# A stated order for top-k, gate softmax, transposes and first router products in a decoder-block kernel

## The chip, the cores and the metric

The kernel runs on one core of one Trainium2 chip. The metric is the time of one execution on the device in microseconds, and the median of several runs is compared. The kernel before takes 1516.3 us (median of 3 runs, 1514.54 to 1518.07).

## What is computed

One decoder block on 512 tokens of width 1024. A joint input projection feeds a gated short convolution and a differential attention; one output projection and a layer norm follow. Behind them stands the channel mixer, a retrieval of 16 out of 16,384 experts for each of 8 heads, and a last layer norm. The change touches the channel mixer alone. Its core, for a chunk of 128 tokens:

```
q = (xc @ wq).reshape(PEER_CHUNK, PEER_HEADS, 2, PEER_DHALF)
sc = jnp.einsum('chpd,hpnd->chpn', q, keys)
s1, i1 = lax.top_k(sc[:, :, 0], PEER_TOPK)
s2, i2 = lax.top_k(sc[:, :, 1], PEER_TOPK)
cand = s1[..., :, None] + s2[..., None, :]             # 16 x 16 per head
cidx = i1[..., :, None] * PEER_NKEYS + i2[..., None, :]
top_s, pos = lax.top_k(cand, PEER_TOPK)
eidx = jnp.take_along_axis(cidx, pos, axis=-1)
g = jax.nn.softmax(top_s, axis=-1)
act = jax.nn.gelu(jnp.einsum('chkd,cd->chk', u[eidx], xc))
return jnp.einsum('chk,chkd->cd', g * act, v[eidx])
```

## The kernel before

The program has four stages: the input projection with attention and convolution, the output projection with the layer norm, the scores against the keys, and the channel mixer. Matrix products that need full precision are made as three products of a high and a low part: ScalarE casts the high part (L72), another engine subtracts for the low part (L73).

The channel mixer treats three of the four token chunks (384 tokens) densely: it computes all 16,384 experts and multiplies by a gate matrix that is zero where an expert wasn't chosen. The fourth chunk gathers its experts' rows. The parts that matter here:

- **Top-k** (`topk`, VectorE). First part: for 8 heads and 2 halves the 16 best of 128 (`top16`, L270 to L274). Second part, from the sums of both halves: the 16 best candidates of each head, the subtraction of the largest (gx, L299), the exp on ScalarE (L300), its sum, reciprocal and product (L302 to L304), then the two index numbers of each choice, found with comparisons and a tree of additions on tiles of 128x2048 (L309 to L331). It is called for chunks 0, 1 and 2 ahead of the expert blocks. The scores of the third chunk come back from DRAM, where ScalarE's evacuations (scst, L409) and stores (L410) have put them.
- **Expert blocks, first half** (`dense_u`, 128 of them). Each loads a weight block of 128x1024, casts it (whi, ScalarE), makes the low part (wlo, on GpSimd for the first NPOOL = 14 blocks, on VectorE for the others), runs 24 products of 128x384 on TensorE into a PSUM tile psH (two buffers) and applies GELU on ScalarE (hs, L432). The results wait in 42 buffers; with two more blocks in psH, 44 blocks can be worked on ahead of the second half.
- **Transposes** (`topk_transpose`): index numbers and gates of a chunk are transposed on TensorE (psX, L337) and evacuated; an edge of the order puts them behind block 3, 10 and 14 (the table TK).
- **Router** (L455 to L473, 24 groups of 16 tokens). VectorE makes one-hot tiles from index numbers and gates (oa, bl, bh, each with two buffers, L462 to L465), TensorE forms 32 products of 128x128 (psG, L470 and L471), ScalarE scales the result into a tile stg, and a transfer stores it in DRAM (G_D, L473).
- **Second half** (`dense_w`, `dense_v`). It reads the gate matrix back from G_D (gt, L553), loads v (vr, L540), multiplies gates and hidden values and accumulates 18 products of 128x512 per block in PSUM tiles acc. The other blocks of the first half stand between them.

A scheduler of the language sets the order of the instructions on each engine from the program's text and from edges that the text adds with `issue_after`; each engine then works through its own list in that order. The transfers of the weights, of v and of the gate matrix stand on SyncE's queue; the stores of G_D and of the scores stand on ScalarE's.

Of the kernel before, what the change touches and what calls it, by code (L numbers as in the profile page):

```python
# [9 lines left out]
F32 = mybir.dt.float32  # L10
# [3 lines left out]
U32 = mybir.dt.uint32  # L14
AF = mybir.ActivationFunctionType
ALU = mybir.AluOpType
AX = mybir.AxisListType
# [7 lines left out]
PH = 8  # L25
# [3 lines left out]
ND = 384  # L29
NDC = 3  # L30
# [7 lines left out]
HS_BUFS = 42  # L38
NPOOL = 14
TAIL = 4  # L40
VR = 3
WB = 4
GA = 4
TK = ((0, 3), (3, 10), (10, 14))
GI2 = 8
# [8 lines left out]
def build(nc, tc, I, out, dbg=None):  # L54
# [13 lines left out]
    SC_D = [dram.tile([128, 16, 128], F32, name=f"SC_D{j}") for j in range(2)]  # L68
# [193 lines left out]
    scs = {}  # L262
# [5 lines left out]
    def top16(tk, vals, pos, src, n):  # L268
        t = tk.tile([128, 128], F32, name="rest", bufs=2)
        nc.vector.max(vals[:, 0:8], src)  # L270
        nc.vector.max_index(pos[:, 0:8], vals[:, 0:8], src)  # L271
        nc.vector.match_replace(t[:, 0:n], vals[:, 0:8], src, -3.0e38)  # L272
        nc.vector.max(vals[:, 8:16], t[:, 0:n])
        nc.vector.max_index(pos[:, 8:16], vals[:, 8:16], t[:, 0:n])  # L274

    def topk(tk, sc, nb):
        m = tk.tile([128, 2, PH, 16], F32, name="m", bufs=nb)
        ix = tk.tile([128, 2, PH, 16], U32, name="ix")
        for h in range(PH):
            for p in range(2):  # L280
                top16(tk, m[:, p, h, :], ix[:, p, h, :], sc[:, 2 * h + p, :], 128)
        ixf = tk.tile([128, 2, 16, PH], F16, name="ixf")
# [12 lines left out]
        for h in range(PH):  # L295
            top16(tk, tsc[:, h, :], pos[:, h, :], cand[:, h, :], 112)
        g = tk.tile([128, 16, PH], F32, name="g", bufs=nb)
        gx = tk.tile([128, PH, 16], F32, name="gx")
# [6 lines left out]
        u1 = tk.tile([128, PH, 16], U32, name="u1")  # L305
        u2 = tk.tile([128, PH, 16], U32, name="u2")
        ab = tk.tile([128, 2, 16, PH], F16, name="ab")
# [3 lines left out]
        nc.vector.scalar_tensor_tensor(abv[:, 0], u2, 12.0, u1, op0=ALU.subtract, op1=ALU.max)  # L311
        u3 = tk.tile([128, PH, 16], U32, name="u3")
        u4 = tk.tile([128, PH, 16], U32, name="u4")
        nc.vector.tensor_scalar(u3, pos, 12, None, op0=ALU.bitwise_and)
        nc.vector.tensor_scalar(u4, pos, 3, None, op0=ALU.bitwise_and)
        nc.vector.scalar_tensor_tensor(u3, pos, 64.0, u3, op0=ALU.is_lt, op1=ALU.mult)
        nc.vector.tensor_tensor(abv[:, 1], u3, u4, op=ALU.add)
        idf = tk.tile([128, 2, 128], F32, name="idf", bufs=nb)
# [9 lines left out]
        for n in (8, 4, 2):  # L328
            nc.vector.tensor_tensor(e[:, :, 0:n], e[:, :, 0:n], e[:, :, n:2 * n], op=ALU.add)  # L329
        nc.vector.tensor_tensor(idf, e[:, :, 0], e[:, :, 1], op=ALU.add)  # L330
        return idf, g  # L331

# [93 lines left out]
    def dense_u(j):  # L426
        uh, ul = wblock(I["uT"][j], nc.gpsimd if j < NPOOL else nc.vector)
        ps = psH.tile([128, S], F32, name="psH")
        for k in range(NK):
            mm = mm3(ps[:, 0:ND], uh[:, k, :], ul[:, k, :], x1h[:, k, 0:ND], x1l[:, k, 0:ND], k == 0, k == NK - 1)  # L430
        hs = hsp.tile([128, ND], F32, name="hs")
        nc.scalar.activation(hs, ps[:, 0:ND], AF.Gelu)  # L432
        hidden[j] = hs
        return mm

    picked = []
    for c in range(NDC):
        if c == 2:
            scs[c] = tk.tile([128, 16, 128], F32, name="sc", bufs=2)
            nc.sync.dma_start(out=scs[c], in_=SC_D[0])  # L440
        picked.append(topk(tk, scs[c], 2))
    for c in range(NDC):
# [12 lines left out]
    for tb in range(NTG):  # L455
# [39 lines left out]
    def gather_steps():  # L495
        with tc.issue_after(gate):
            idf, g = topk(t3, sc3, 1)
        for p in range(2):
# [153 lines left out]
```

## Time and profile before

| What | Value |
|---|---|
| Median of 3 runs | 1516.3 us (1514.54 to 1518.07) |
| Profiled execution | 1515.57 us, its span 1513.8 us |
| Mean granted clock of TensorE | 0.985 |
| DMA, mean over the span | 248 GB/s |

The span is the time between the first and the last instruction of the profiled execution; the remaining 1.8 us lie around it. A busy share is the time in which an engine had an instruction in work, over the span. The engines are PE (TensorE), PEld (its weight loads), DVE (VectorE), ACT (ScalarE), POOL (GpSimd) and SP (SyncE). In the page's slices the channel mixer begins in the tenth of 40 slices, at some 360 us, and its second half in the seventeenth, at some 626 us.

### The profile page before, as it was taken

The numbers are of one execution on the slowest core, as the hardware profiler recorded it, in microseconds if no ns is written. First come the engines' busy times: TensorE is split into PE (matmuls) and PEld (weight loads), VectorE is DVE, ScalarE is ACT, GpSimd is POOL, SyncE is SP. The second block draws the span as 40 slices with busy tenths as digits, with TensorE's granted clock in tenths as the row PEclk, the third lists the DMA queues.
The fourth block names the chain that finished last, engine by engine and source line by source line (L and its number), as shares of the span: only waits on it lengthen the run. The fifth ranks groups of instructions, "written<-read, shape, count | busy, mean of one in ns | idle before, by whom it ended". The sixth has DMA issues, their size and how long they took to land.

```text
span 1513.8 us, 22123 instructions
## 1 busy us (share of the span) xinstructions
PE 1452.1 (96%) x8097; PEld 1299.5 (86%) x8097; DVE 1183.8 (78%) x2373; ACT 592.9 (39%) x932; POOL 476.7 (31%) x322
## 2 busy tenths in 40 slices
PE   7999988997799999899999999999999999999996
PEld 5787867997798999888989999899899999998985
DVE  4546545579999887699888888888888888888745
ACT  3544244452345555334433333333333333333342
POOL 1000043674430000000345454445444544444200
PEclk9999999999899999999999999999999999999999
DMA  6111263454436666996799999999999999999731
GB/s 254 62 65 58 96 208 131 156 197 131 139 130 228 242 233 250 298 295 193 264 377 339 350 334 346 344 333 344 334 357 329 350 333 344 334 340 346 275 126 70
DMA packets 146429, 375.94 MB, mean 248 GB/s; under 512 B 16272, under 2 KB 63376, under 8 KB 142992
## 3 DMA queue, kind: packets, MB, share of 16 engines
q1 hardware_dynamic: 100960, 203.97, 39.8%
q0 software_dynamic: 36864, 134.23, 24.3%
q10 hardware_dynamic: 8496, 36.32, 6.3%
q8 instruction: 63, 1.03, 0.3%
q14 instruction: 46, 0.38, 0.1%
HBM read 343.55 MB, written 30.93 MB: 247 GB/s over the span
## 4 chain that ended last, share of the span: by engine, by line
PE 82%; DVE 12%; DMA 3%; ACT 1%; issue 1%; SPq 0%; POOL 0%; ACTq 0%; DVEq 0%; POOLq 0%
PE psH L86 14%; PE psH L84 14%; PE psH L85 14%; PE acc L84 11%; PE acc L85 11%; PE acc L86 11%; PE psG L470 1%; PE psS L180 1%; PE psG L471 1%; DVE rest L272 1%; DVE sc L325 1%; DMA raw<-w_out 1%; DVE sc L329 1%; DVE ix L274 1%; DVE ix L271 1%
## 5 line engine op out<-in xcount | busy, mean ns | idle before, releaser
L84 PE MATMUL psH<-x1Th,whi 128*128 128x384 f32 (+1 forms) x1280 | 423.7, 331 | 15.0 <-ACT hs L432 15.0
L86 PE MATMUL psH<-x1Th,wlo 128*128 128x384 f32 (+1 forms) x1280 | 423.0, 330 | 3.7 <-DVE wlo L73 2.5
L85 PE MATMUL psH<-x1Tl,whi 128*128 128x384 f32 (+1 forms) x1280 | 420.9, 329 | 0.0
L72 ACT CAST whi<-raw 128x1024 fp32r<-128x1024 f32 x200 | 209.7, 1050 | 435.9 <-PE psH L85 313.6
L508 POOL DMA_INDIRECT row<-u,idx x128 | 169.5, 1324 | 457.8 <-ACT hs L432 290.3
L85 PE MATMUL acc<-vl,wh 128*128 128x512 f32 x756 | 294.4, 389 | 0.0
L86 PE MATMUL acc<-vh,wl 128*128 128x512 f32 x756 | 294.3, 389 | 0.0
L84 PE MATMUL acc<-vh,wh 128*128 128x512 f32 x756 | 288.9, 391 | 4.4 <-ACT vh L72 4.4
L84 PEld LDWEIGHTS psH<-x1Th,whi 128*128 128x128 f32 x1280 | 243.9, 191 | 19.3 <-ACT hs L432 15.7
L73 DVE TENSOR_TENSOR wlo<-raw,whi 128x1024 fp32r<-128x1024 f32 x146 | 180.0, 1233 | 92.1 <-ACT whi L72 90.6
L86 PEld LDWEIGHTS psH<-x1Th,wlo 128*128 128x128 f32 x1280 | 243.9, 191 | 5.7 <-DVE wlo L73 3.4
L85 PEld LDWEIGHTS psH<-x1Tl,whi 128*128 128x128 f32 x1280 | 244.1, 191 | 3.2
L73 POOL TENSOR_TENSOR wlo<-raw,whi 128x1024 fp32r<-128x1024 f32 x54 | 136.0, 2522 | 300.7 <-ACT whi L72 299.8
L508 POOL DMA_INDIRECT row<-v,idx x128 | 166.1, 1298 | 183.7 <-DVE x L523 136.2
L72 ACT CAST wh<-hs 128x384 fp32r<-128x384 f32 x128 | 65.6, 514 | 322.1 <-PE acc L85 318.2
L84 PEld LDWEIGHTS acc<-vh,wh 128*128 128x128 f32 x756 | 142.2, 188 | 30.9 <-ACT vh L72 4.8
L86 PEld LDWEIGHTS acc<-vh,wl 128*128 128x128 f32 x756 | 142.0, 188 | 29.0
L73 DVE TENSOR_TENSOR vl<-vr,vh 128x1024 fp32r<-128x1024 f32 x126 | 154.3, 1224 | 16.0 <-ACT vh L72 15.7
L523 DVE SCALAR_TENSOR_TENSOR x<-row,gw,x 128x1024 f32<-128x1024 f32 x128 | 164.0, 1281 | 3.5 <-DMA row<-v,idx 2.6
L85 PEld LDWEIGHTS acc<-vl,wh 128*128 128x128 f32 x756 | 142.0, 188 | 26.0
L516 DVE SCALAR_TENSOR_TENSOR row<-row,x 128x1024 f32<-128x1024 f32 x128 | 154.7, 1221 | 10.7 <-DMA row<-u,idx 10.7
L72 ACT CAST vh<-vr 128x1024 fp32r<-128x1024 f32 x126 | 131.9, 1048 | 0.1
(196 smaller groups left out, 1668.5 us busy)
## 6 DMA issues: line engine op xcount, KB each, us to landing
raw<-uT SPq DMA_DIRECT2D x128, 512.0 KB, 5.4
vr<-v SPq DMA_DIRECT2D x128, 512.0 KB, 5.4
G_D<-stg ACTq DMA_DIRECT2D x24, 1024.0 KB, 4.7
gt<-G_D SPq DMA_DIRECT2D x46, 512.0 KB, 7.9
raw<-wq SPq DMA_DIRECT2D x32, 512.0 KB, 3.4
raw<-w_in SPq DMA_DIRECT2D x24, 512.0 KB, 3.4
raw<-w_out SPq DMA_DIRECT2D x16, 512.0 KB, 4.7
xr<-xT SPq DMA_DIRECT2D x4, 512.0 KB, 6.5
```

The lines of the kernel that those rows point to most:

```text
L72: nc.scalar.copy(out=hi, in_=raw)
L73: return sub.tensor_sub(lo, raw, hi.bitcast(F32))
L84: nc.tensor.matmul(ps, lh, rh, start=first, stop=False)
L85: nc.tensor.matmul(ps, lh, rl, start=False, stop=False)
L86: return nc.tensor.matmul(ps, ll, rh, start=False, stop=last)
L180: nc.tensor.matmul(sp[:, p, 0:w], qz[:, h, p, qs], kT[:, h, 0:w], start=True, stop=False)
L271: nc.vector.max_index(pos[:, 0:8], vals[:, 0:8], src)
L272: nc.vector.match_replace(t[:, 0:n], vals[:, 0:8], src, -3.0e38)
L274: nc.vector.max_index(pos[:, 8:16], vals[:, 8:16], t[:, 0:n])
L508: ins = nc.gpsimd.indirect_dma_start(out=t, out_offset=None, in_=I["uv"[p]], in_offset=bass.IndirectOffsetOnAxis(ap=idx[:, p, k:k + 1], ax ...
L516: nc.vector.scalar_tensor_tensor(t, t, 1.0, x1, op0=ALU.mult, op1=ALU.mult, accum_out=dots[:, k:k + 1])
L523: nc.vector.scalar_tensor_tensor(x1, t, gw[:, k:k + 1], x1, op0=ALU.mult, op1=ALU.add, accum_out=tots[:, GCH:GCH + 1] if k == 127 else None)
```

## The change

The number of blocks whose low part GpSimd makes rises from 14 to 18. The exp of the gates and the sum, reciprocal and product behind it leave `topk` for a function `gates`. For the first two chunks the exps are issued behind the GELU of block 10, sum and product behind the first part of the third chunk's top-k; for the third chunk they come behind block 18 and its own top-k. The transposes are put behind block 12, 13 and 20, and all router products behind the last product of block 18. The first ten blocks now stand in the text between the top-k of the second and of the third chunk. Four index tiles share the memory of ix.

```diff
-NPOOL = 14
+NPOOL = 18
...
-TK = ((0, 3), (3, 10), (10, 14))
+GATES_AT = (10, 18)
+TRANSPOSE_AT = (12, 13, 20)
+ROUTER_AT = 18
...
-    def topk(tk, sc, nb):
-        m = tk.tile([128, 2, PH, 16], F32, name="m", bufs=nb)
+    def topk(tk, sc, nb, between=None):
+        m = tk.tile([128, 2, PH, 16], F32, name="m", bufs=min(nb, 2))
...
+                ins = top16(tk, m[:, p, h, :], ix[:, p, h, :], sc[:, 2 * h + p, :], 128)
+        if between:
+            with tc.issue_after(between(ins)):
+                return topk_rest(tk, sc, nb, m, ix)
+        return topk_rest(tk, sc, nb, m, ix)
...
-        nc.scalar.activation(gx, gx, AF.Exp)
-        gs = tk.tile([128, PH], F32, name="gs")
-        nc.vector.tensor_reduce(gs, gx, axis=AX.X, op=ALU.add)
-        nc.vector.reciprocal(gs, gs)
-        nc.vector.tensor_tensor(g.rearrange("p k h -> p h k"), gx, gs.unsqueeze(2).broadcast_to([128, PH, 16]), op=ALU.mult)
...
+    def gates(tk, gxs, nb, last, exp_after=None):
+        gt = []
+        with tc.issue_after(exp_after) if exp_after else ExitStack():
+            for gx in gxs:
+                nc.scalar.activation(gx, gx, AF.Exp)
+        with tc.issue_after(last.ins):
+            for gx in gxs:
+                g = tk.tile([128, 16, PH], F32, name="g", bufs=nb)
+                gs = tk.tile([128, PH], F32, name="gs", bufs=2)
+                nc.vector.tensor_reduce(gs, gx, axis=AX.X, op=ALU.add)
+                nc.vector.reciprocal(gs, gs)
+                ins = nc.vector.tensor_tensor(g.rearrange("p k h -> p h k"), gx, gs.unsqueeze(2).broadcast_to([128, PH, 16]), op=ALU.mult)
+                gt.append(g)
+        return gt, ins.ins
...
+    picked = [topk(tk, scs[c], NDC) for c in range(2)]
+    scs[2] = tk.tile([128, 16, 128], F32, name="sc", bufs=2)
+    nc.sync.dma_start(out=scs[2], in_=SC_D[0])
+    for j in range(GATES_AT[0]):
+        _, act = dense_u(j)
+    gt = []
+
+    def first_gates(ins):
+        g, last = gates(tk, [gx for _, gx, _ in picked], NDC, ins, act.ins)
+        gt.extend(g)
+        return last
+
+    picked.append(topk(tk, scs[2], NDC, first_gates))
     for c in range(NDC):
-        for j in range(*TK[c]):
-            mm = dense_u(j)
+        for j in range(j + 1, TRANSPOSE_AT[c]):
+            mm, act = dense_u(j)
+            if j == ROUTER_AT - 1:
+                router = mm.ins
+            if j == GATES_AT[1] - 1:
+                gt.extend(gates(tk, [picked[2][1]], NDC, picked[2][2], act.ins)[0])
         with tc.issue_after(mm.ins):
-            topk_transpose(c, *picked[c])
+            topk_transpose(c, picked[c][0], gt[c])
...
-            for t in range(4):
-                q = o0 + t
-                nc.tensor.matmul(ps[:, t, :], oa[:, q, :], bh[:, q, :], start=True, stop=False)
-                nc.tensor.matmul(ps[:, t, :], oa[:, q, :], bl[:, q, :], start=False, stop=True)
+            with tc.issue_after(router):
+                for t in range(4):
+                    q = o0 + t
+                    nc.tensor.matmul(ps[:, t, :], oa[:, q, :], bh[:, q, :], start=True, stop=False)
+                    nc.tensor.matmul(ps[:, t, :], oa[:, q, :], bl[:, q, :], start=False, stop=True)
```

What this does to the lists of the engines is seen at three places.

ScalarE, around the end of the scores. Before, with the exp of the second chunk (gx, L300) ahead of the cast and the last evacuation of scores:

```order
L395 COPY qT<-psH 128x256
L300 ACTIVATE gx<-gx 128x128
L72 CAST whi<-raw 128x1024
L409 COPY scst<-psT 128x512 x2
L410 DMA SC_D_70<-scst 128x512
L410 DMA SC_D_71<-scst 128x512
L432 ACT_TABLE_LOAD
L432 ACTIVATE hs<-psH 128x384
```

With the change, behind the GELU of block 10 (L446 was L432, L336 was L300, L74 was L72):

```order
L446 ACTIVATE hs<-psH 128x384
L336 ACT_TABLE_LOAD
L336 ACTIVATE gx<-gx 128x128 x2
L74 CAST whi<-raw 128x1024
L446 ACT_TABLE_LOAD
L446 ACTIVATE hs<-psH 128x384
```

Both exps now stand behind ten GELUs, with two table loads around them. A place in the list of its own remains to the exp of the third chunk, behind block 18.

VectorE, at the first splits of weights (wlo) that it makes in the channel mixer. Before, for block 15, with one-hots of the router already around it:

```order
L321 TENSOR_TENSOR sc<-ab,iota_1507 128x2048
L304 TENSOR_TENSOR g<-gx,gs 128x8x16
L73 TENSOR_TENSOR wlo<-raw,whi 128x1024
L325 TENSOR_TENSOR sc<-sc,ixf 128x2048
L329 TENSOR_TENSOR sc<-sc 128x2x1024
L462 TENSOR_TENSOR oa<-iox,iT 128x2048
L463 TENSOR_TENSOR bl<-iox,iT 128x2048
L329 TENSOR_TENSOR sc<-sc 128x2x512
L73 TENSOR_TENSOR wlo<-raw,whi 128x1024
```

With the change, for block 19 (L75 was L73, L320, L324 and L328 were L321, L325 and L329):

```order
L320 TENSOR_TENSOR sc<-ab,iota_1507 128x2048
L324 TENSOR_TENSOR sc<-sc,ixf 128x2048
L328 TENSOR_TENSOR sc<-sc 128x2x1024
L75 TENSOR_TENSOR wlo<-raw,whi 128x1024
L328 TENSOR_TENSOR sc<-sc 128x2x512
L328 TENSOR_TENSOR sc<-sc 128x2x256
L329 TENSOR_TENSOR idf<-sc 128x256
L75 TENSOR_TENSOR wlo<-raw,whi 128x1024
```

The first split now stands behind the comparisons, the products and the first addition of the third chunk's tree. Ahead of it one router group's four one-hot operations stand fewer than before.

TensorE, around the last router product (psG) ahead of the second half. Before:

```order
L470 MATMUL psG_5340<-bh_5304,oa_5303 128x128
L471 LDWEIGHTS oa_5303
L471 MATMUL psG_5340<-bl_5305,oa_5303 128x128
L85 MATMUL psH_6237<-x1Tl_1497,whi_6232 128x384
L86 MATMUL psH_6237<-x1Th_1496,wlo_6233 128x384
L84 MATMUL psH_6270<-x1Th_1496,whi_6265 128x384
```

With the change (L496 and L497 were L470 and L471):

```order
L496 MATMUL psG_5526<-bh_5490,oa_5489 128x128
L497 LDWEIGHTS oa_5489
L497 MATMUL psG_5526<-bl_5491,oa_5489 128x128
L86 MATMUL acc0_5547<-vh_6292,wh_6300 128x512
L86 MATMUL acc1_5548<-vh_6292,wh_6300 128x512
L86 MATMUL acc2_5549<-vh_6292,wh_6300 128x512
```

Before, the last 74 expert products of the first half's 44 blocks (1056 products) stand behind the last router product and ahead of the first acc; with the change all 1056 stand ahead of it, and the last 158 router products of 768 stand behind the last expert product. Ahead of the first router product stand 170 expert products before and 432 with the change; the router products stand in 79 runs between expert products before and in 67 with the change.

## Rows read from the trace of the kernel before

**Rows 1.** The page, busy time, share of the span and instructions of each engine:

```profile
PE 1452.1 (96%) x8097; PEld 1299.5 (86%) x8097; DVE 1183.8 (78%) x2373; ACT 592.9 (39%) x932; POOL 476.7 (31%) x322
```

**Rows 2.** Waits of TensorE: engine, line waited for, us in total, times, longest us:

```profile
PE psH L84 <- ACT hs L432: 15.0, 1, 15.0
...
PE psG L470 <- DVE bh L464: 4.2, 1, 4.2
```

**Rows 3.** ScalarE's timeline: start us, us, line, operation, tiles, [idle before <- releaser]:

```profile
378.69 0.31 ACT L300 ACTIVATE gx<-gx 128x128 f32<-128x128 f32 x1 [17.15 <-DVE gx L299]
...
382.67 1.28 ACT L432 ACT_TABLE_LOAD   x1 [1.77 <-DMA SC_D<-scst]
```

**Rows 4.** Windows: us, engines' busy time (count), TensorE's granted clock, DMA share, GB/s:

```profile
384.50:390.00 5.50, 5.49 (x17) 5.50 (x18) 5.50 (x6) 1.28 (x2) 2.82 (x1) 0.50 0.78 302
413.00:417.50 4.50, 4.49 (x19) 4.48 (x19) 4.50 (x12) 0.00 (x0) 0.00 (x0) 0.62 0.34 117
626.00:629.00 3.00, 2.94 (x8) 2.44 (x9) 3.00 (x15) 1.72 (x4) 0.00 (x0) 0.50 1.12 342
```

**Rows 5.** TensorE's timeline, expert products at 360, 390 and 451 to 457 us:

```profile
360.46 0.42 PE L84 MATMUL psH<-x1Th,whi 128*128 128x384 f32 x1
...
390.32 0.34 PE L84 MATMUL psH<-x1Th,whi 128*128 128x384 f32 x1
...
391.19 0.34 PE L86 MATMUL psH<-x1Th,wlo 128*128 128x384 f32 x1
...
450.92 0.45 PE L86 MATMUL psH<-x1Th,wlo 128*128 128x384 f32 x1 [1.53 <-DVE wlo L73]
...
457.32 0.44 PE L86 MATMUL psH<-x1Th,wlo 128*128 128x384 f32 x1 [0.99 <-DVE wlo L73]
```

**Rows 6.** TensorE's timeline, a run of ten router products between two expert products:

```profile
443.24 0.34 PE L85 MATMUL psH<-x1Tl,whi 128*128 128x384 f32 x1
...
443.88 0.22 PE L471 MATMUL psG<-bl,oa 128*128 128x128 f16 x1
...
444.22 0.34 PE L84 MATMUL psH<-x1Th,whi 128*128 128x384 f32 x1
```

**Rows 7.** TensorE's timeline, last router, last expert and first acc product:

```profile
608.51 0.22 PE L471 MATMUL psG<-bl,oa 128*128 128x128 f16 x1
...
621.28 0.34 PE L86 MATMUL psH<-x1Th,wlo 128*128 128x384 f32 x1
...
626.06 1.65 PE L84 MATMUL acc<-vh,wh 128*128 128x512 f32 x3 [4.44 <-ACT vh L72]
```

**Rows 8.** The chain of waits, 608 to 627 us: start us, us, what:

```profile
609.44 4.82 DMA G_D<-stg
...
618.98 4.74 DMA vr<-v
```

**Rows 9.** VectorE's timeline, third chunk's top-k, operations beside GpSimd's, last one-hots:

```profile
330.59 2.40 DVE L309 TENSOR_SCALAR u<-pos 128x128 uint32<-128x128 uint32 x1
...
345.04 2.59 DVE L304 TENSOR_TENSOR g<-gx,gs 128x128 f32<-128x128 f32 x1
...
436.34 2.53 DVE L464 TENSOR_TENSOR bh<-bl,gT 128x2048 f16<-128x2048 f16 x1
...
443.69 0.26 DVE L299 TENSOR_TENSOR gx<-tsc 128x128 f32<-128x128 f32 x1
...
449.44 0.38 DVE L304 TENSOR_TENSOR g<-gx,gs 128x128 f32<-128x128 f32 x1
...
452.03 1.23 DVE L329 TENSOR_TENSOR sc<-sc 128x2048 f16<-128x2048 f16 x1
...
594.67 1.22 DVE L462 TENSOR_TENSOR oa<-iox,iT 128x2048 f16<-128x2048 f16 x1
595.81 1.22 DVE L463 TENSOR_TENSOR bl<-iox,iT 128x2048 f16<-128x2048 f16 x1
```

**Rows 10.** GpSimd's timeline, the split behind its longest pause here:

```profile
380.01 3.28 POOL L73 TENSOR_TENSOR wlo<-raw,whi 128x1024 fp32r<-128x1024 f32 x1 [16.27 <-ACT whi L72]
```

More of the change, by code (lines that the diff above doesn't have):

```diff
@@ L273, in top16 @@
         nc.vector.max(vals[:, 8:16], t[:, 0:n])
-        nc.vector.max_index(pos[:, 8:16], vals[:, 8:16], t[:, 0:n])
-    def topk(tk, sc, nb):
-        m = tk.tile([128, 2, PH, 16], F32, name="m", bufs=nb)
+        return nc.vector.max_index(pos[:, 8:16], vals[:, 8:16], t[:, 0:n])
+    def topk(tk, sc, nb, between=None):
+        m = tk.tile([128, 2, PH, 16], F32, name="m", bufs=min(nb, 2))
         ix = tk.tile([128, 2, PH, 16], U32, name="ix")
@@ L280, in topk, with topk_rest @@
             for p in range(2):
-                top16(tk, m[:, p, h, :], ix[:, p, h, :], sc[:, 2 * h + p, :], 128)
+                ins = top16(tk, m[:, p, h, :], ix[:, p, h, :], sc[:, 2 * h + p, :], 128)
[3 more added lines that the diff above has]
+        return topk_rest(tk, sc, nb, m, ix)
+    def topk_rest(tk, sc, nb, m, ix):
         ixf = tk.tile([128, 2, 16, PH], F16, name="ixf")
@@ L296, in topk @@
             top16(tk, tsc[:, h, :], pos[:, h, :], cand[:, h, :], 112)
-        g = tk.tile([128, 16, PH], F32, name="g", bufs=nb)
-        gx = tk.tile([128, PH, 16], F32, name="gx")
+        gx = tk.tile([128, PH, 16], F32, name="gx", bufs=nb)
         nc.vector.tensor_tensor(gx, tsc, tsc[:, :, 0:1].broadcast_to([128, PH, 16]), op=ALU.subtract)
-        nc.scalar.activation(gx, gx, AF.Exp)
-        gs = tk.tile([128, PH], F32, name="gs")
-        nc.vector.tensor_reduce(gs, gx, axis=AX.X, op=ALU.add)
-        nc.vector.reciprocal(gs, gs)
-        nc.vector.tensor_tensor(g.rearrange("p k h -> p h k"), gx, gs.unsqueeze(2).broadcast_to([128, PH, 16]), op=ALU.mult)
-        u1 = tk.tile([128, PH, 16], U32, name="u1")
-        u2 = tk.tile([128, PH, 16], U32, name="u2")
+        u1, u2 = ix[:, 0], ix[:, 1]
         ab = tk.tile([128, 2, 16, PH], F16, name="ab")
@@ L311, in topk @@
         nc.vector.scalar_tensor_tensor(abv[:, 0], u2, 12.0, u1, op0=ALU.subtract, op1=ALU.max)
[L312 to L317, printed above, removed]
+        nc.vector.tensor_scalar(u1, pos, 12, None, op0=ALU.bitwise_and)
+        nc.vector.tensor_scalar(u2, pos, 3, None, op0=ALU.bitwise_and)
+        nc.vector.scalar_tensor_tensor(u1, pos, 64.0, u1, op0=ALU.is_lt, op1=ALU.mult)
+        nc.vector.tensor_tensor(abv[:, 1], u1, u2, op=ALU.add)
         idf = tk.tile([128, 2, 128], F32, name="idf", bufs=nb)
@@ L329, in topk @@
             nc.vector.tensor_tensor(e[:, :, 0:n], e[:, :, 0:n], e[:, :, n:2 * n], op=ALU.add)
-        nc.vector.tensor_tensor(idf, e[:, :, 0], e[:, :, 1], op=ALU.add)
-        return idf, g
+        ins = nc.vector.tensor_tensor(idf, e[:, :, 0], e[:, :, 1], op=ALU.add)
+        return idf, gx, ins
+    def gates(tk, gxs, nb, last, exp_after=None):
[12 more added lines that the diff above has]
+        return gt, ins.ins
     def topk_transpose(c, idf, g):
@@ L431, in dense_u @@
         hs = hsp.tile([128, ND], F32, name="hs")
-        nc.scalar.activation(hs, ps[:, 0:ND], AF.Gelu)
+        act = nc.scalar.activation(hs, ps[:, 0:ND], AF.Gelu)
         hidden[j] = hs
-        return mm
-    picked = []
-    for c in range(NDC):
[L438 to L442, printed above, removed]
-        for j in range(*TK[c]):
-            mm = dense_u(j)
+        return mm, act
+    picked = [topk(tk, scs[c], NDC) for c in range(2)]
[9 more added lines that the diff above has]
+    picked.append(topk(tk, scs[2], NDC, first_gates))
+    for c in range(NDC):
+        for j in range(j + 1, TRANSPOSE_AT[c]):
[4 more added lines that the diff above has]
+                gt.extend(gates(tk, [picked[2][1]], NDC, picked[2][2], act.ins)[0])
         with tc.issue_after(mm.ins):
-            topk_transpose(c, *picked[c])
+            topk_transpose(c, picked[c][0], gt[c])
     g_ctx = ExitStack()
@@ L496, in gather_steps @@
         with tc.issue_after(gate):
-            idf, g = topk(t3, sc3, 1)
+            idf, gx, ins = topk(t3, sc3, 1)
+            (g,), _ = gates(t3, [gx], 1, ins)
         for p in range(2):
```

## The prediction

> **What bounds the kernel now.** I read the page's busy shares first. TensorE is busy 1452.1 of 1513.8 us, VectorE 1183.8 [rows 1], so TensorE sets the time, and a change is worth what it adds to or takes from TensorE's idle and slow stretches. The waits of TensorE come next: of some 60 us that it isn't busy the longest single wait is 15.0 us, for ScalarE's GELU at L432, and there is one of 4.2 us for VectorE's one-hot tiles [rows 2]. Both stand in the stretch that the change touches, so all else is read there: from the first expert block's first product at 360.46 us to the first product of the second half (acc, L84) at 626.06 us.
>
> ScalarE's timeline tells what the 15.0 us are. An exp of gate values (gx, L300) stands on its queue between two casts; it was issued at once, waited 17.15 us for VectorE's top-k of the second token chunk, and everything behind it waited too, the evacuations of TensorE's PSUM tiles among them [rows 3]. TensorE then ran its next 17 products in 5.50 us, at a granted clock of 0.50, the lower of the two levels (1.2 GHz) [rows 4]; at full clock a product takes 0.174 us from start to start (five in 0.87 us) [rows 5]. So the wait cost 15.0 + 17 x (0.32 - 0.174) = 17.5 us. The wait for the first one-hots cost 4.2 and, with a clock of 0.62 over 4.5 us behind it [rows 4], some 1.5 more. Two waits for a low-part split on VectorE (L73) add 1.5 + 1.0 [rows 5]. In all 25.7 us that this stretch could lose.
>
> As a check, TensorE's own work up to the last router product: 982 expert products x 0.174 = 170.4; 768 router products at 0.056 and, for each of their 79 runs between expert products, 0.08 for the switch (ten of them lie in 443.24 to 444.22 beside two normal steps: 0.98 - 0.35 = 0.63 [rows 6]), so 42.7 + 6.3; transposes and four key products 1.3. That is 220.7, with the waits 246.4. The trace has 608.51 - 360.46 = 248.1 [rows 5, 7]; 1.6 stay unexplained and are left as they are.
>
> **The change, part by part.** The exps of the first two chunks go behind block 10's GELU, their sums and products behind the first half of the third chunk's top-k. All waits above go away: **-25.7**.
>
> What stood in their shadow comes out. Before, three expert blocks stood behind the last router product. They ran from 608.5 to 621.6 us, while that product's result went through an eviction, the store to G_D, its read back and the load of v, until the first acc product at 626.06: 17.5 us, of which TensorE idled only 4.4 [rows 7, 8]. Now all 1056 expert products stand ahead of the last router product and nothing is left for that path: 74 x 0.174 = 12.9 earlier work, less 12 fewer runs x 0.08: **+11.9**. The path itself has the same steps.
>
> The table load ahead of block 1's GELU still waits for the store of the last scores (1.77 us [rows 3]), since its tile takes their memory. Without the stall TensorE gets there first and waits about **+1.1** (0 to 2).
>
> Next is a new wait. Block 19 is the first whose split is VectorE's, and in VectorE's order that split stands behind the third chunk's last top-k, deep in its second part. When is it done? The subtraction that starts that part (gx, L299) is at 443.69 now. Ahead of it one one-hot group fewer (4 x 1.14 = 4.5; 594.67 to 595.81 is one operation), no held-up product of the first chunk's gates (2.59 against 0.38 undisturbed, here 2.2), and no held-up bh of the third group (1.4): 435.6. From there to the end of the first tree addition (452.03 + 1.1 - 443.69 = 9.4, less 1.6 for a split and a gate that stand there no longer) 7.8, and the split 1.1: 444.5 [rows 9]. TensorE is at block 19's third product at 360.46 + 0.4 + 432 x 0.174 + 0.7 (two groups of transposes) + 0.3 + 1.1 + 0.3 = 438.4. I take **+6.1**, and **+1.5** for the clock behind it, as behind the wait of 4.2. The bounds are 0 (VectorE escapes most of GpSimd's holds) and 11 (it meets more of them), the clock 0 to 2.5 (the 17 products above).
>
> GpSimd now makes 18 of the splits, and no pause of 16 us [rows 10] is left in which VectorE has the memory alone. What that does is seen where VectorE's operations on two SBUF tensors meet one: a shift took 2.40 us, the gate product 2.59 instead of 0.38, a one-hot 2.53 instead of 1.22 [rows 9]; each ended as GpSimd's operation did. The Trainium skill, "SBUF — State Buffer", section "Who interferes with whom", calls the shared ports an exclusive lock under which the second to issue fully blocks until the first has finished. By that rule, and the trace agrees, four more splits of 2.4 us on GpSimd can take up to 9.6 us from VectorE and save it 4 x 1.14 = 4.6; it speaks against this part of the change. The sum has them as equal; the other reading is the third rival.
>
> The last term is the tail. A one-hot tile has two buffers, so group 22 of 24 can't begin before group 20's products are done, and in the new order those stand just ahead of the last expert block's end. From there VectorE needs 3 groups and a split, 13 x 1.14 = 14.8, and TensorE 1.6 more for the last products; TensorE alone would need 8.0 for what it has left. **+8.4** (5 to 10), with bursts between idle spells, so that the last products run at the lower clock: **+1.6** (0 to 2). The store path then finds TensorE idle for 17 us instead of 4.4. Behind 4.4 us it ran 3.0 us at a granted clock of 0.50, behind 15 us 5.5 [rows 4]; half of the difference: **+1.2**.
>
> Behind the first acc product the orders keep pace (the same expert blocks stand ahead of each acc product to within a few), and TensorE stays the bound. The other edits (gates out of the middle of top-k, reused index tiles) remove no work; they lie on VectorE under TensorE's blocks, and cost a like amount if that cover is gone.
>
> Sum: -25.7 + 11.9 + 1.1 + 6.1 + 1.5 + 8.4 + 1.6 + 1.2 = +6.1, on the profiled execution's 1515.6: 1521.7. The median of the three runs stands 0.7 above that execution, so **1522 us**.
>
> **The rivals.** First, TensorE alone is the bound: neither the split for block 19 nor the one-hots of the tail are late. For it speaks that VectorE began its last group's one-hots 13.8 us ahead of the last router product before (594.67 against 608.51 [rows 7, 9]), against it that it did so because TensorE had waited 25.7 us. Then 6.1, 1.5, 8.4 and 1.6 fall away: 1522 - 17.6 = 1504, **faster**. It decides at group 22: if its first one-hot starts before the last expert block ends, this one holds.
>
> Second, only the tail is late: VectorE reaches block 19's split by 438 us, since its top-k of the first chunks loses less to GpSimd. Then 7.6 fall away: 1514, no change that a measurement can tell. That the exps are moved and the stretch gives it all back is the same outcome.
>
> Third, GpSimd's denser splits hold VectorE more: the split comes 5 us later, at the upper bound of 11, the clock costs 1 more: 1528.
>
> **How the numbers follow.** The forecast has 0.50 (its own range is 1518 to 1526), the first rival 0.12, the second 0.23, the third 0.15. About 0.2%, 3 us, is what a measurement of this kernel can tell from no change: 1513.3 to 1519.3. The first rival and a fifth of the second are faster: 0.17. The rest of the second and the low end of the forecast, 0.07, are the same: 0.26. The others are slower: 0.57. The range is 1512 to 1529: it leaves out the first rival and a little above the third.
>
> **What would show it.** Right: no wait of ScalarE for gx over 2 us; TensorE waiting 4 to 9 us for wlo, L75, near 440 us; the last expert block's products ended before the last three groups of router products, which come some 4.5 us apart; then 17 us idle up to the first acc product, near 632 us. Wrong: no wait at block 19, or the last router product ahead of 604 us.

## The result and the profile after

The change makes the kernel slower: 1529.95 us (median of 4 runs, 1527.82 to 1530.92) against 1515.8 us before (4 runs), a ratio of 1.0085 with a 95% interval of 1.0069 to 1.0100. That is 14 us where 6 were forecast, and 1 us above the range. The profiled execution took 1530.92 us, 1.0 above its median; its span is 1529.2 us, 15.4 longer than before. The page's first section answers to [rows 1]: TensorE does the same work and idles more.

```profile
PE 1452.7 (95%) x8097; PEld 1301.2 (85%) x8097; DVE 1186.7 (78%) x2369; ACT 595.2 (39%) x933; POOL 475.4 (31%) x326
```

Where the 15.4 us lie is read from TensorE's timeline of the change, which answers to [rows 5, 7] (L86 to L88 were L84 to L86, L496 and L497 were L470 and L471):

```profile
362.21 0.42 PE L86 MATMUL psH<-x1Th,whi 128*128 128x384 f32 x1
...
374.25 0.44 PE L86 MATMUL psH<-x1Th,whi 128*128 128x384 f32 x1 [3.01 <-ACT hs L446]
...
421.44 0.33 PE L352 MATMUL psX<-ident,g 128*128 128x128 f32 x1 [3.45 <-DVE g L343]
...
435.43 0.66 PE L351 MATMUL psX<-ident,idf 128*128 128x128 f32 x2 [5.32 <-DVE gT L357]
...
457.59 0.45 PE L88 MATMUL psH<-x1Th,wlo 128*128 128x384 f32 x1 [1.86 <-DVE wlo L75]
...
606.27 0.34 PE L88 MATMUL psH<-x1Th,wlo 128*128 128x384 f32 x1
...
610.47 0.34 PE L496 MATMUL psG<-bh,oa 128*128 128x128 f16 x3 [1.80 <-DVE bh L489]
613.87 0.27 PE L497 MATMUL psG<-bl,oa 128*128 128x128 f16 x1 [3.06 <-DVE bl L490]
620.83 0.34 PE L496 MATMUL psG<-bh,oa 128*128 128x128 f16 x3 [1.37 <-DVE bh L489]
622.09 0.22 PE L497 MATMUL psG<-bl,oa 128*128 128x128 f16 x1 [0.91 <-DVE bl L490]
...
623.71 0.22 PE L497 MATMUL psG<-bl,oa 128*128 128x128 f16 x1
...
641.01 1.65 PE L86 MATMUL acc<-vh,wh 128*128 128x512 f32 x3 [17.07 <-DMA vr<-v]
```

The first expert product comes at 362.21 instead of 360.46. These 1.75 us arise in the first 35 us, at the loads of the input, which the change doesn't touch. So runs are compared by **the stretch** from the first expert product to the first acc product: 265.6 us before, 641.01 - 362.21 = 278.8 after, 13.2 more. Behind it the difference is 0.45 (1529.2 - 641.01 against 1513.8 - 626.06).

The waits of [rows 2, 5] are gone. In their place stand waits for VectorE at the transposes (3.45 and 5.32 us) and a smaller one at block 19's split; then come the waits of the tail and 17.07 us of idle time up to the first acc. What the waits do to the clock is seen in the windows, whose columns are those of [rows 4]. TensorE ran 17 instructions in the ten microseconds around the second wait at the transposes, at a mean granted clock of 0.66; in the 4.6 us right behind that wait it was 0.50, the lower level. The tail has a mean of 0.66 too, and the stretch behind the first acc the lower level.

```profile
430.00:440.00 10.00, 4.68 (x17) 4.60 (x17) 10.00 (x18) 2.54 (x6) 2.41 (x1) 0.66 0.32 105
435.40:440.00 4.60, 4.57 (x16) 4.60 (x17) 4.60 (x9) 1.11 (x4) 0.00 (x0) 0.50 0.20 77
...
610.00:620.00 10.00, 5.83 (x64) 5.41 (x64) 8.98 (x9) 4.18 (x8) 0.00 (x0) 0.66 0.64 223
641.00:644.00 3.00, 2.99 (x8) 2.71 (x9) 3.00 (x13) 1.65 (x3) 0.00 (x0) 0.50 1.21 292
```

VectorE's timeline tells why TensorE waits at the transposes. The tile psX has one buffer, so the second chunk's transposes wait until the first chunk's gT (L357) has left it. In VectorE's list gT stands behind the start of the third chunk's second part and two one-hots, one of which is held beside a split of GpSimd's (3.36 against 1.23 us): the operation is in work, but does its part only when the split has ended. The gate subtraction gx and L315 are held behind it, and seven operations ahead of it, from L297 on (in the row of L328 two of three).

```profile
367.75 2.72 DVE L297 TENSOR_TENSOR sc<-m 128x384 f32<-128x384 f32 x1
...
380.22 0.27 DVE L306 TENSOR_TENSOR gx<-tsc 128x128 f32<-128x128 f32 x1
...
381.57 2.19 DVE L313 TENSOR_SCALAR ix<-pos 128x128 uint32<-128x128 uint32 x1
...
386.30 2.94 DVE L316 TENSOR_TENSOR ab<-ix 128x128 f16<-128x128 uint32 x1
...
390.53 3.31 DVE L324 TENSOR_TENSOR sc<-sc,ixf 128x2048 f16<-128x2048 f16 x1
393.88 6.80 DVE L328 TENSOR_TENSOR sc<-sc 128x2048 f16<-128x2048 f16 x3
...
420.37 1.25 DVE L343 TENSOR_TENSOR g<-gx,gs 128x128 f32<-128x128 f32 x2
...
430.13 1.23 DVE L487 TENSOR_TENSOR oa<-iox,iT 128x2048 f16<-128x2048 f16 x1
431.27 3.36 DVE L488 TENSOR_TENSOR bl<-iox,iT 128x2048 f16<-128x2048 f16 x1
434.81 0.47 DVE L357 SCALAR_TENSOR_TENSOR gT<-psX,gT 128x128 f16<-128x128 f32 x2
...
443.99 1.87 DVE L306 TENSOR_TENSOR gx<-tsc 128x128 f32<-128x128 f32 x1
...
448.35 2.48 DVE L315 SCALAR_TENSOR_TENSOR ix<-pos,ix 128x128 uint32<-128x128 uint32 x1
...
456.31 1.22 DVE L75 TENSOR_TENSOR wlo<-raw,whi 128x1024 fp32r<-128x1024 f32 x1
```

GpSimd's split beside the one-hot at 431.27:

```profile
431.14 2.41 POOL L75 TENSOR_TENSOR wlo<-raw,whi 128x1024 fp32r<-128x1024 f32 x1 [1.76 <-ACT whi L74]
```

One number on the change above is wrong: 126 router products stand behind the last expert product, not 158.

### The profile page after: what moved, and what is told of

Its sections match the earlier page's. It is cut to its first block, busy times and chain, and to the rows that moved or that the text cites. A ratio compares the mean times of both kernels' runs of the same rounds, so it can differ in the third digit from the quotient of the medians.

```text
span 1529.2 us, 22123 instructions
## 1 busy us (share of the span) xinstructions
PE 1452.7 (95%) x8097; PEld 1301.2 (85%) x8097; DVE 1186.7 (78%) x2369; ACT 595.2 (39%) x933; POOL 475.4 (31%) x326
## 4 chain that ended last, share of the span: by engine, by line
PE 82%; DVE 13%; DMA 3%; ACT 1%; issue 1%; SPq 0%; POOL 0%; ACTq 0%; DVEq 0%; POOLq 0%
PE psH L88 14%; PE psH L86 14%; PE psH L87 14%; PE acc L86 11%; PE acc L88 11%; PE acc L87 11%; PE psG L497 1%; PE psG L496 1%; PE psS L182 1%; DVE rest L274 1%; DVE sc L324 1%; DVE sc L328 1%; DMA raw<-w_out 1%; DMA raw<-w_in 1%; DVE ix L273 1%
## 5 line engine op out<-in xcount | busy, mean ns | idle before, releaser
L86 PE MATMUL psH<-x1Th,whi 128*128 128x384 f32 (+1 forms) x1280 | 422.7, 330 | 3.0 <-ACT hs L446 3.0
L88 PE MATMUL psH<-x1Th,wlo 128*128 128x384 f32 (+1 forms) x1280 | 422.2, 330 | 3.1 <-DVE wlo L75 1.9
L74 ACT CAST whi<-raw 128x1024 fp32r<-128x1024 f32 x200 | 209.9, 1050 | 439.3 <-PE psH L87 301.0
L535 POOL DMA_INDIRECT row<-u,idx x128 | 163.6, 1278 | 468.4 <-PE psH L88 296.5
L86 PE MATMUL acc<-vh,wh 128*128 128x512 f32 x756 | 288.4, 390 | 17.1 <-DMA vr<-v 17.1
L88 PE MATMUL acc<-vh,wl 128*128 128x512 f32 x756 | 294.1, 389 | 0.0
L86 PEld LDWEIGHTS psH<-x1Th,whi 128*128 128x128 f32 x1280 | 244.1, 191 | 6.9 <-ACT hs L446 3.3
L88 PEld LDWEIGHTS psH<-x1Th,wlo 128*128 128x128 f32 x1280 | 243.7, 190 | 4.5 <-DVE wlo L75 2.0
L75 DVE TENSOR_TENSOR wlo<-raw,whi 128x1024 fp32r<-128x1024 f32 x142 | 175.4, 1235 | 88.6 <-ACT whi L74 81.7
L75 POOL TENSOR_TENSOR wlo<-raw,whi 128x1024 fp32r<-128x1024 f32 x58 | 143.6, 2479 | 301.1 <-ACT whi L74 301.1
L74 ACT CAST wh<-hs 128x384 fp32r<-128x384 f32 x128 | 65.6, 514 | 335.5 <-PE acc L87 312.4
L86 PEld LDWEIGHTS acc<-vh,wh 128*128 128x128 f32 x756 | 142.1, 188 | 43.4 <-ACT vh L74 17.2
L88 PEld LDWEIGHTS acc<-vh,wl 128*128 128x128 f32 x756 | 141.9, 188 | 29.1
L75 DVE TENSOR_TENSOR vl<-vr,vh 128x1024 fp32r<-128x1024 f32 x126 | 153.9, 1221 | 15.4 <-ACT vh L74 13.4
L74 ACT CAST vh<-vr 128x1024 fp32r<-128x1024 f32 x126 | 132.1, 1048 | 0.0
```

The source lines that it names most:

```text
L74: nc.scalar.copy(out=hi, in_=raw)
L75: return sub.tensor_sub(lo, raw, hi.bitcast(F32))
L86: nc.tensor.matmul(ps, lh, rh, start=first, stop=False)
L88: return nc.tensor.matmul(ps, ll, rh, start=False, stop=last)
L535: ins = nc.gpsimd.indirect_dma_start(out=t, out_offset=None, in_=I["uv"[p]], in_offset=bass.IndirectOffsetOnAxis(ap=idx[:, p, k:k + 1], ax ...
```

## The experiments

All ratios are to the kernel before, run beside each kernel, where it took 1515.05 to 1517.63 us; "stretch" is that of the kernel's one profiled execution. Two rows whose intervals overlap are not told apart by their times.

| Run | us | ratio, 95% interval | stretch, us |
|---|---|---|---|
| before | 1515.8 | | 265.6 |
| the change | 1529.95 | 1.0085 (1.0069 to 1.0100) | 278.8 |
| one_exp | 1521.33 | 1.0031 (1.0013 to 1.0050) | 272.7 |
| trans_late | 1527.19 | 1.0070 (1.0051 to 1.0089) | 276.7 |
| np14 | 1525.79 | 1.0051 (1.0034 to 1.0067) | 274.4 |
| np6 | 1531.16 | 1.0100 (1.0073 to 1.0127) | 278.9 |
| no_pool | 1515.98 | 0.9990 (0.9978 to 1.0003) | 266.8 |
| pieces | 1512.44 | 0.9966 (0.9952 to 0.9979) | 272.4 |
| before_p | 1500.95 | 0.9907 (0.9890 to 0.9924) | 259.7 |
| no_edge | 1527.24 | 1.0078 (1.0049 to 1.0108) | 276.6 |
| cover | 1527.02 | 1.0068 (1.0046 to 1.0090) | 273.3 |
| mix | 1517.29 | 1.0005 (0.9990 to 1.0020) | 268.6 |
| mix14 | 1516.83 | 0.9995 (0.9977 to 1.0012) | 264.9 |
| mix14p | 1501.75 | 0.9897 (0.9868 to 0.9927) | 262.2 |
| best1 | 1525.89 | 1.0070 (1.0047 to 1.0093) | 277.9 |
| best2p | 1507.24 | 0.9940 (0.9923 to 0.9956) | 271.8 |

### Who is late ahead of block 19

**one_exp**, on the kernel before (the function holds the exp, sum, reciprocal and product):

```diff
+EXP_AT = 6
...
+            if j == EXP_AT - 1:
+                with tc.issue_after(act.ins):
+                    softmax(tk, *picked[1][1:])
+                picked.append(topk(tk, scs[2], 2))
```

> The kernel before with one edit: the exp of the second chunk's gates stands behind block 6's GELU instead of among the casts, its sum and product where VectorE comes to them; transposes, router order and GpSimd's share are as before. If the 15.0 us wait and the lower clock behind it were a loss by themselves, 17.5 us go: about 1499 us. If VectorE is the bound from 360 to 450 us (theory), TensorE comes to the first router product some 15 us earlier and waits there instead: 1511 to 1516, with a wait for the first one-hots of 10 to 20 us where 4.2 stood.

The wait for the exp fell from 15.0 to 2.0 us, and TensorE's waits (us in total, times, longest) show what came for it:

```profile
PE psG L475 <- DVE bh L469: 19.3, 1, 19.3
```

Before, 4.2 us stood at this product. So the 17.5 us that the prediction booked as a gain were not free: TensorE came sooner to a point that VectorE sets. The first router product came 52.1 us after the first expert product, and 52.6 before. The run is even slower than the 1511 to 1516 expected. Its list leaves 34 expert products instead of 74 behind the last router product, which comes 7.2 us later; the way from there to the first acc is as long as before (17.4 us), and TensorE stands idle for 11.2 us of it instead of 4.4.

**trans_late:**

```diff
-TRANSPOSE_AT = (12, 13, 20)
+TRANSPOSE_AT = (15, 18, 20)
```

> The change with the transposes of chunk 1 and 2 put behind block 15 and 18 instead of 12 and 13. If the two waits at the transposes (3.45 and 5.32 us, with the lower clock behind them about 11 us) are a cost of that place, they go and the time falls to about 1519 us. If VectorE's top-k of the third chunk is the bound there and TensorE only waits for it at another place (theory), the wait moves to the first split that VectorE makes, at block 19, which grows from 1.9 to some 10 us, and the time stays at 1526 to 1531.

The wait moved, though to the later transposes and not to the split, as TensorE's timeline shows:

```profile
445.49 0.66 PE L351 MATMUL psX<-ident,idf 128*128 128x128 f32 x2 [7.84 <-DVE gT L357]
```

The stretch fell by 2.1 us, 1.1 of them at the table load (1.91 instead of 3.01), and the time can't be told from the change's. Where a wait for VectorE stands in TensorE's list matters little.

### What holds VectorE

**np14** and **np6** set NPOOL to 14 and 6, with all else as in the change.

> The change with GpSimd making the splits of 14 blocks, as before, instead of 18. If GpSimd's splits hold VectorE by some 2.2 us each and so delay the third chunk's top-k (theory, in part), VectorE gains 4 x 2.2 and loses 4 x 1.1 for its own splits: 1524 to 1528. If it is the order alone, no change: 1528 to 1532.

> The change with GpSimd making 6 splits instead of 18. If each split of GpSimd holds VectorE by about 2.2 us (theory), VectorE gains 26 us of holds and spends 14 us on its own splits: the waits at the transposes shrink by up to 10 us, and the time is some 1520 to 1524. If VectorE's splits for blocks 7 to 18 stand behind its top-k in its list (rival), TensorE waits for them instead, and the time is 1530 or more.

np14 fell by 4.2 us to the middle of its range, but only in part for the reason given. VectorE's third gate subtraction comes 79.7 us after the first expert product, 81.8 in the change. The order of TensorE's list changed as well: 104 router products stand behind the last expert product, 126 in the change, the last two waits for one-hots (1.37 and 0.91 us) are gone, and the way from the last expert product to the last router product is 3.3 us shorter. np6 and no_pool have these 104 too.

np6 went the rival's way, though its time can't be told from the change's: VectorE's list puts its split for an early block behind top-k, and TensorE waited 14.2 us for it (us in total, times, longest):

```profile
PE psH L88 <- DVE wlo L75: 15.8, 3, 14.2
```

Less work for GpSimd is a gain only while no split has to stand in the middle of VectorE's top-k.

**no_pool** takes the holds away without giving VectorE the work. It leaves out the low part of the first 18 blocks' weights; TensorE makes as many products as before:

```diff
+    def high_only(src):
...
+        nc.scalar.copy(out=hi, in_=raw)
+        return hi, hi
...
-        uh, ul = wblock(I["uT"][j], nc.gpsimd if j < NPOOL else nc.vector)
+        uh, ul = high_only(I["uT"][j]) if j < NPOOL else wblock(I["uT"][j], nc.vector)
```

> The change with the splits of the first 18 expert blocks left out: the high part stands in for the low part, which leaves out the low part of these weights, and GpSimd does nothing between 362 and 460 us. If GpSimd's splits hold VectorE (theory: 8 holds, 15.6 us, ahead of the third chunk's gate subtraction, 3.8 us more behind it), the subtraction stands some 15 us after the first expert product sooner (at 66 instead of 82 us), the waits of 3.45, 5.32 and 1.86 us all but vanish, and the time is 1513 to 1518; the tail stays as it is. If the order of the lists makes these waits (rival), the time is 1526 to 1530.

1516.0 us, and the three waits are gone. The gate subtraction comes 69.7 us after the first expert product (429.16 - 359.49), 81.8 in the change; the stretch is 12.0 us shorter. From TensorE's timeline and from VectorE's:

```profile
359.49 0.42 PE L86 MATMUL psH<-x1Th,whi 128*128 128x384 f32 x1
```

```profile
429.16 0.28 DVE L306 TENSOR_TENSOR gx<-tsc 128x128 f32<-128x128 f32 x1
```

So GpSimd's splits, not the order alone, made the waits of the middle. Some 2 of the 12.0 us of the stretch belong to the tail, where the last two waits are missing. The subtraction comes 12 us sooner and not 15 because VectorE then waits itself, 7.24 us for the two exps behind block 10 (the sum of their gates starts at 411.49).

**pieces** leaves all work where it is and shortens GpSimd's instructions:

```diff
+        if sub is nc.gpsimd:
+            for a in range(0, 8, 2):
+                ins = sub.tensor_sub(lo[:, a:a + 2], raw[:, a:a + 2], hi.bitcast(F32)[:, a:a + 2])
+            return ins
```

> The change with each of GpSimd's splits written as four subtractions of a quarter. If VectorE is held only until GpSimd's instruction in work has ended (theory), a hold shrinks from 2.2 to some 0.6 us, VectorE reaches the third chunk's gate subtraction some 10 us sooner (72 instead of 82 us after the first expert product), and the time is 1516 to 1522. If a held operation waits until GpSimd has nothing left to do (rival), or four instructions cost GpSimd much more than one, the time stays at 1526 or more.

17.5 us less than the change, faster than the kernel before and below the expected range. The same one-hot beside GpSimd, in VectorE's timeline:

```profile
409.23 1.23 DVE L491 TENSOR_TENSOR oa<-iox,iT 128x2048 f16<-128x2048 f16 x1
410.37 1.76 DVE L492 TENSOR_TENSOR bl<-iox,iT 128x2048 f16<-128x2048 f16 x1
```

The second is held for 0.53 us where the change held it for 2.13. It is held by the quarter in work, which ends at 411.05, and not by the next ones:

```profile
409.64 1.41 POOL L77 TENSOR_TENSOR wlo<-raw,whi 128x256 fp32r<-128x256 f32 x1 [1.68 <-ACT whi L74]
```

The Trainium skill, "SBUF — State Buffer", section "Who interferes with whom", states that the engine that issues first has the shared ports for its whole instruction and that the other is blocked; the trace agrees, with these two holds. GpSimd pays for the shorter holds: four pieces take 5.92 us where VectorE's operations come between, against 2.4 us for one whole split.

Some 12 of the 17.5 us lie ahead of the stretch, and the expectation didn't count them: the first expert product comes at 349.3 us, 12.9 sooner, of which 0.8 arise at the loads of the input; the output projection and the scores have splits on GpSimd too. In the stretch the gain is 6.4 us. VectorE enters it 11 us ahead (the second chunk's gate subtraction comes 7.0 us after the first expert product, 18.0 in the change), but then stands idle for 10.35 us, waiting for the exps behind block 10, so that the third chunk's subtraction comes after 74.4 us, where 72 were expected. GpSimd's row:

```profile
361.51 5.92 POOL L77 TENSOR_TENSOR wlo<-raw,whi 128x256 fp32r<-128x256 f32 x4 [3.77 <-ACT whi L74]
```

**before_p** makes the same edit in the kernel before.

> The kernel before with each of GpSimd's splits in four pieces, as in pieces. The 12 us ahead of the first expert product go here too. If the change's order is a loss by itself, through its tail (theory: 22 us of tail and store path against 26 us of waits that short holds shrink in any order), this is 1498 to 1505, clearly below the 1512 of pieces. If the holds were the whole difference (rival), it is 1509 to 1514.

1501.0 us, 11.5 below pieces (0.6%, or 9 us, by the ratios): with short holds on both sides the change's order still loses. Its stretch is 12.7 us longer (272.4 against 259.7). In pieces TensorE waits 17.5 us at the first acc and 6.6 in the tail ahead of it, nearly all for one-hots, in before_p 11.3 and nothing: 12.8. The waits ahead of the tail are shorter in pieces than in before_p (7.0 against 9.7 us), so what the order loses here is the tail. TensorE's longest wait in before_p:

```profile
PE acc L88 <- ACT vh L72: 11.3, 1, 11.3
```

### The tail

**no_edge** drops the edge that puts router products behind block 18.

> The change without the edge that puts the router products behind block 18: 360 instead of 432 expert products stand ahead of the first router product and 94 instead of 126 router products behind the last expert product. The tail is 32 products shorter, but VectorE's one-hots pace it: 2 to 4 us less in the tail, and no loss in the middle if VectorE is the bound there, so 1525 to 1528. If the edge shields TensorE from a wait for the first one-hots (rival), that wait appears near 430 us and the time is 1530 to 1535.

It lies where the theory put it, 2.7 us below the change, which the intervals can't tell from no difference; of the wait that the edge might have shielded 0.74 us appears. What is refuted is the rival's 1530 to 1535.

**cover** and **mix** put expert blocks back behind the last router product, cover with a whole block behind each group, mix with quarters of a block behind 8 router products (steps is a generator of a block's quarters):

```diff
+        if tb >= 2:
+            dense_u(len(hidden), pg.ins)
```

```diff
-            with tc.issue_after(router):
+            with tc.issue_after(router if tb < 3 else order[-1]):
...
+            if tb >= 3:
...
+                    order.append(steps.send(mm.ins))
```

> The change with one edit: each of the expert blocks 21 to 42 is put behind the last product of one router group (groups 3 to 24), so that 72 expert products stand behind the last router product, as 74 did before. If the tail is the cost (theory: some 9 us of waits for one-hots and 13.8 us more of idle time on the store path), the stretch from the first expert product to the first acc falls from 278.8 to some 256 us and the time to about 1508 us. If VectorE's one-hots set the end of the router products whatever TensorE's order is (rival), the last router product stays near 623 us and the time stays at 1526 to 1530.

> The change with one edit: router groups 4 to 24 and expert blocks 21 to 41 take turns on TensorE, four times a quarter of a block behind 8 router products; 78 expert products stand behind the last router product. The run cover still waited 0.48 us ahead of each group's last evacuation and shorter times ahead of the others, 6.67 us per group and block; here 6.3 are expected. With the first 458 us as in the change, the last router product comes at about 600 us, the first acc near 616, the time near 1506 us. If VectorE can't make a group and a split in 6.3 us (rival), waits for bh or bl come in every group and the time stays above 1515.

Both missed, cover by 19 us. In cover the 32 router products of a group stand in one row, and each group waits for ScalarE's evacuations of psG; in TensorE's timeline two groups follow 6.66 us apart:

```profile
611.08 0.22 PE L497 MATMUL psG<-bh,oa 128*128 128x128 f16 x1 [0.48 <-ACT stg L499]
...
617.74 0.22 PE L497 MATMUL psG<-bh,oa 128*128 128x128 f16 x1 [0.48 <-ACT stg L499]
```

In mix a group and a block take 6.26 us without a wait, as worked out, and the last router product comes 247.6 us after the first expert product, 261.5 in the change; 600 - 362 = 238 were expected. What I left out: TensorE waits for VectorE at groups 3 and 4 (1.16 and 3.06 us) before the pairs begin, and the last store of G_D takes 8.73 us, 5.22 in the change, as the chain of waits has it (start us, us, what):

```profile
607.17 8.73 DMA G_D<-stg
```

Loads of weights, the reload of scores and the store before it run beside that store in mix; which of them slows it isn't shown. Still, mix takes back 12.7 of the change's 14 us, and 10.2 of the 13.2 in the stretch, though its waits in the middle remain (12.0 us up to block 19, 13.6 in the change). So most of what the change loses lies in the tail.

**mix14** and **mix14p** are mix with 14 splits on GpSimd, and that with the splits in pieces.

> The run mix with GpSimd making 14 splits instead of 18. np14 was 4.2 us faster than the change; if that is VectorE's time up to block 19 it adds up here: some 4 us below mix, near 1502 us. If the tail of the change had hidden or caused that gain, the two are equal.

> The run mix14 with GpSimd's splits in four pieces each. With the holds shortened as in pieces, TensorE's waits of 4.1, 1.9, 3.7, 1.2, 3.9 and 1.8 us up to group 4 shrink by 8 to 12 us in all: 1505 to 1509, faster than the kernel before. If the holds don't shrink (rival), 1515 to 1518.

mix14 is the same as mix in time (1516.8 and 1517.3), so the 4.2 us of np14 didn't add up. At block 19's third product, the first that reads the low part, the two differ by 0.6 us (92.4 and 93.0 after the first expert product). mix14's stretch is 3.7 us shorter, but most of that arises behind block 19, and its first expert product comes 4.4 us later, so the effect of four splits on the time is left open. mix14p is below its expected range, faster than the kernel before, and within the uncertainty equal to before_p, which needs one edit only.

**best1** and **best2p** run 24 blocks ahead of the paired part and 18 instead of 24 expert products to a group; best2p has the first router product behind block 24 and the pieces.

> A version built from the runs so far: 24 blocks stand ahead of the paired part and are split by GpSimd, so that TensorE has products while VectorE ends the third chunk's top-k; transposes behind block 14, 22 and 24; from group 4 on every 8 router products are followed by 3 or 6 expert products (18 to a group), so that 108 expert products stand behind the last router product and cover the store path. If VectorE can make a group and 0.75 split in 5.5 us (theory), the last router product comes some 228 us after the first expert product instead of 261 and the first acc some 248 us after it instead of 279: about 1500 us. If VectorE is later by the holds of six more GpSimd splits (rival), 1506 to 1512.

> The run best1 with the first router product behind block 24 instead of 18 and GpSimd's splits in pieces. If the wait of 11.8 us for the first one-hots came from that place, it goes, and with the 12 us ahead of the first expert product and VectorE some 8 us earlier the time is 1485 to 1497. If VectorE's 5.9 us per group are the bound from group 4 on (rival), it is 1500 to 1508, no better than mix14p.

best1 missed both ranges: its list kept the first router product at block 18, and TensorE waited 11.8 us for one-hots that had not begun. In best2p that wait is gone, but VectorE waits in turn, 7.12 us for the third chunk's exp and 6.87 for the transposes, which stand behind block 20 and 22; from group 5 on a group takes 6.0 us, with a wait of 2.4 for bl every fourth group. The rival held. VectorE's row:

```profile
445.87 0.29 DVE L347 TENSOR_REDUCE gs<-gx 128x8 f32<-128x128 f32 x1 [7.12 <-ACT gx L342]
```

## Why the prediction was wrong

Two points of the sum can be set against the trace. Block 19's third product was forecast at 444.5, 84.0 us after the first expert product; it came after 457.59 - 362.21 = 95.4. The first acc was forecast after 265.6 + 4.9 = 270.5 (the sum of 6.1 less the 1.2 that lie behind it); it came after 278.8. So the stretch was 11.3 us late at block 19 and 8.3 at its end: the error arose ahead of block 19. One execution tells the first of these to some 3 us only; cover and mix, whose text is the change's up to block 20, have that product after 92.4 and 93.0.

- **"The sum has them as equal"** belongs to the step that failed, VectorE's way to block 19's split. The forecast took over the holds by GpSimd's splits from the kernel before, took two of them away (2.2 and 1.4 us), put none in their place and set the four extra splits at nothing. From the first expert product to that split it so kept 10.9 us of holds; the change has ten, 19.4 us in all.

  Counted from the first expert product, the second chunk's gate subtraction stands where it stood (380.22 - 362.21 = 18.0 against 378.37 - 360.46 = 17.9): the 2.2 that were to go there came back as a hold at L297 (2.72 us instead of 0.5). From there to the third chunk's subtraction VectorE before has seven holds, 12.3 us in all, of which the forecast kept 10.9. The first six, beside the one at 436.34 [rows 9]:

```profile
378.37 0.28 DVE L299 TENSOR_TENSOR gx<-tsc 128x128 f32<-128x128 f32 x1
...
381.00 2.86 DVE L317 TENSOR_TENSOR ab<-u,u 128x128 f16<-128x128 uint32 x1
...
386.09 3.28 DVE L325 TENSOR_TENSOR sc<-sc,ixf 128x2048 f16<-128x2048 f16 x1
...
402.27 2.63 DVE L463 TENSOR_TENSOR bl<-iox,iT 128x2048 f16<-128x2048 f16 x1
...
406.23 3.14 DVE L463 TENSOR_TENSOR bl<-iox,iT 128x2048 f16<-128x2048 f16 x1
...
409.81 3.14 DVE L464 TENSOR_TENSOR bh<-bl,gT 128x2048 f16<-128x2048 f16 x1
...
425.52 2.15 DVE L289 TENSOR_TENSOR sc<-m 128x384 f32<-128x384 f32 x1
```

  The change has seven there too, of 2.0, 2.2, 2.1, 2.2, 2.2, 0.6 and 2.15, 13.4 in all. A further 1.9 us are the first chunk's sum, reciprocal and product, which now stand in this part (some 0.6), and operations that overlap less with their neighbours. That is 2.2 + 2.5 + 1.9 = 6.6 us late, and the subtraction stands at 81.8 where 435.6 - 360.46 = 75.1 was forecast. Behind it two more holds (1.6 at gx, 2.2 at L315) make up most of the other 4.7.

  no_pool and pieces show the holds to be a cause. np14 prices the four extra splits by themselves: without them VectorE has six holds up to block 19's split, 11.3 us in all, close to the 10.9 that the forecast kept. So the four brought 8.1 us of holds (5.3 in mix, which has 16.6) against 4 x 1.14 = 4.6 of work that they took from VectorE: they weren't equal. At the third chunk's subtraction it is 4.3 us of holds against two splits, 2.3: np14 gets there 2.1 us sooner than the change. The third rival named the mechanism, at a chance of 0.15 and 1528 us.
- **The place of the wait** was wrong too. The transposes were priced as 0.7 us of work; that their tile has one buffer, and that VectorE's gT frees it from behind one-hots, wasn't costed. TensorE waited 8.8 us there and only 1.86 at block 19, where 6.1 was forecast (6.4 and 3.9 us in mix). trans_late shows that the place hardly matters, the lateness of VectorE does.
- **-25.7** came as forecast in the list of waits and was no gain: VectorE sets when TensorE passes the third chunk's top-k. one_exp takes the largest part of it away by itself, and the time doesn't fall. A sum of waits taken from one engine's view holds only while the engine it waits for next isn't the bound.
- **+1.1** for the table load: 3.01 in this execution, above the bounds of 0 to 2; 1.7 to 1.9 in trans_late, np14, cover and mix, inside them.
- **+11.9 and +8.4**, the tail, were right. TensorE waited 1.80 + 3.06 + 1.37 + 0.91 us for one-hots, and 17.07 for the store path, forecast as 17. Of the 17.4 us between the last expert and the last router product some 3 are neither work at full clock nor a wait; they go with the lower clock, forecast as 1.6. From the last router product to the first acc it is 17.2 to 17.5 us in the kernel before, one_exp, before_p and the change, with 74, 34, 32 and no expert products on the way. mix, which undoes the tail alone, gains 12.7 us, and before_p stands 11.5 below pieces.
- **+1.2** for the clock behind the first acc: all that lies behind it is 0.45 longer.

Three slips of the prediction changed little. 982 x 0.174 is 170.9 and not 170.4, which leaves some 1.1 us of its check unexplained instead of 1.6. The 126 router products behind the last expert product take 126 x 0.056 = 7.1 us of TensorE and not 8.0, which makes the +8.4 a +9.3. And the held operations of [rows 9] didn't end as GpSimd's did but ran behind them: the split that held the bh at 436.34 ended at 437.79, the bh at 438.87.

The first rival (1504) is refuted by the tail's waits for bh and bl, the second (1514) by the 11.3 us at block 19. The sign set for the first rival misled: group 22's first one-hot began at 605.78, just ahead of the end of the last expert product (606.27 + 0.34), and TensorE waited even so.

## What to carry to other kernels

A wait that is taken away is a gain only if the engine waited for isn't the bound a little further on: before summing up waits, follow the other engine's list to the next point where both meet. Where two engines exclude each other by instruction, cut the longer instructions; four quarters in place of one took 14 us off the kernel before (1500.95 against 1515.05 beside it), more than any order of the lists here did; some 11 of them lie ahead of the first expert product. And an operation moved out of a quiet place is to be priced with everything that stands beside it in the new one.

## What the runs showed of the hardware

A hold of VectorE ends with GpSimd's instruction in work, not with GpSimd's queue: 0.53 us beside quarter splits and 2.13 beside whole ones, with the next quarters still to come. GpSimd is held in its turn: in pieces the quarter that issued at 411.01, behind that one-hot, took 1.72 us, where one with nothing beside it took 0.73.
